# A two-layer diffusion backbone on one core: the first stage of layer 0 gets more places and a merged scale-and-shift pass, and layer 1 computes its input projection with tokens as rows

## The chip, the cores and the metric

The kernel runs on one core of a Trainium2 chip. The engines are TensorE (PE, with its weight loads PEld shown apart), VectorE (DVE), ScalarE (ACT), GpSimd (POOL) and SyncE (SP). SP issues nearly all transfers. The metric is device time of one execution in microseconds. The kernel before has a median of 1796.73 us over three runs (1795.94 to 1799.53).

## The reference, cut to what matters

The input is a latent stream `x` of 256 tokens by 2048 channels, a context stream of the same size and a conditioning vector. Two layers follow each other. Layer 0 mixes with neighbourhood attention and a bidirectional state-space scan, layer 1 with a gated short convolution:

```
for i in range(DEPTH):                                   # DEPTH = 2
    shift, scale, gate = adaln(c, ada_w[i], ada_b[i])
    h = modulate(rms_norm(x, norm_g[i]), shift[:, None], scale[:, None])
    ...
    if i % 2 == 0:  y, yc = na_ssd_mixer(h, hc, ...)     # layer 0
    else:           y = short_conv_mixer(h, sc_w_in, sc_conv_w, sc_w_out)
    x = x + gate[:, None] * y

def short_conv_mixer(h, w_in, conv_w, w_out):
    p = h @ w_in                                         # 256 x 2048 @ 2048 x 8192
    bg, cg, hv, g = jnp.split(p, 4, axis=-1)
    y = bg * dw_conv(cg * hv, conv_w)                    # 3 taps along the tokens
    return (jax.nn.silu(g) * y) @ w_out                  # 2048 x 2048
```

All of it is float32. Shift and scale of layer 0 are needed for the latent stream and for the context stream.

## The kernel before

**Split products.** Each float32 operand of a large product is split into a high part, rounded to the fp32r type, and a low part, the remainder. A product is then three matmuls: high by high, high by low, low by high. Weights arrive by transfers of 512 KB (`raw`, 128 x 1024), ACT makes the high part (`split`, L407) and DVE the low part (`low_part`, L414). There are three places (`NW = 3`) for split weights, used in turn, and five `raw` buffers; during the first stage four more tiles (`spare`: PT0, PT1, xtm, yi) serve as `raw` as well.

**Two forms of a product.** Every matmul is recorded on L189 and every transpose on L193; the profile's names read out<-moving,stationary. In the "act" form (`mm_act`) a 128 x 128 block of activations is stationary, 512 weight columns move, and the result has tokens as partitions: three matmuls of 512 columns for each block of 128 channels, 128 tokens and 512 outputs. In `mm_ws` the weights are stationary. `mm_both` is a variant of it that only layer 1 uses: activations' high and low parts for all 256 tokens lie side by side in one tile of 512 columns, so one matmul of 512 columns with the high weights and one of 256 with the low weights serve a block of 128 channels and 128 outputs. The result has channels as partitions, with the two halves of the bank still to be added (`both`, L1771 and L1773).

**Order of the work.** A planner (`Plan`) keeps a modelled clock of each engine and of the transfers (`RATE`, in bytes per ns) while the program is written out. Generators (`ada_gen`, `res_gen`, `norm_gen` and so on) yield what they wait for, and `pump` or `force` emits their next instructions once the model says that these are ready. The result is one fixed order per engine, and each engine runs its own order strictly in sequence. `keys` says which piece of a tile an access touches, for the model's dependences.

**First stage (L700 to L899).** Eight steps `j`, each for 256 of the 2048 input channels. A step needs its scale and shift: `ada_gen` multiplies the padded conditioning vectors by eight `raw` loads, four for the scale and four for the shift, each part with a bank, an ACT copy, two transposes and a DVE reduction of its own. Then it builds `hH` and `hL` (scaled input, high and low), and PE runs the K, V and Q columns in the act form and the B columns with stationary weights. K and V are summed over the steps on DVE (`part_gen`, L776).

**From layer 0 to layer 1 (L1564 to L1755).** The output projection of layer 0 runs in three passes over 16 chunks; the first pass has two column blocks of 512 and takes its four banks at once. In the last pass the last three chunks (`NTAIL = 13`) are run for tokens 0 to 127 first and then for tokens 128 to 255. `res_gen` forms the residual `x1` and its squares, `turn_gen` transposes `x1` to channels by tokens, `norm_gen` forms the root mean square of each token, spreads it over the partitions with a transpose (bank `rb`), and makes the normalised `h1` channel block by channel block for all 256 tokens together. Two sets of dummy transposes (`keep_up`) run on PE meanwhile. Layer 1's first matmul waits for the first `h1`.

**Layer 1 (L1757 to L1855).** For each of four channel groups `i` the parts 1, 2, 0, 3 of `sc_in` are projected with `mm_both` into four banks, and `cg_gen`, `hv_gen`, `bg_gen` and `gg_gen` do the gating and the convolution in the channel-major layout. Then the output projection runs in the act form, and `fin_gen` writes the result.

Of the kernel before, what the change touches and what calls it, by code (L numbers as in the profile page):

```python
# [15 lines left out]
KB = 16  # L16
# [21 lines left out]
class Plan:  # L38
# [3 lines left out]
    RATE = 270.0  # L42
# [7 lines left out]
    def keys(self, ap):  # L50
        a, n = ap.ap, ap.tensor.name
        if type(ap.tensor).__name__ == "Tile" and not n.startswith("dram"):
            lo = ap.offset % a[0][0] if a[0][0] else ap.offset
            hi = lo + sum(abs(s) * (c - 1) for s, c in a[1:])
            return [(n, u) for u in range(lo // 128, hi // 128 + 1)]
# [86 lines left out]
def kernel(ctx: ExitStack, tc, x, cx, ada0, ada_w, ada_b, w_in, w_out, sc_in, sc_out, rpb, small, const,  # L142
# [27 lines left out]
    KT, QT, Vt, gt = st([128, 4, 512], "KT", F32R), st([128, 4, 256], "QT", F32R), st([128, 4, 512], "Vt"), st([128, 4, 256], "gt")  # L170
    KL, QL = st([128, 4, 512], "KL", F32R), st([128, 4, 256], "QL", F32R)
# [3 lines left out]
    spare = [t.rearrange("p a b -> p (a b)") for t in (PT[0], PT[1], xtm, yi)]  # L175
# [212 lines left out]

    def split():
        k = pos["split"]  # L390
        raw, v = RAW.pop(k)
        nb, n = v.shape[1], v.shape[2]
        if n == 64:
# [3 lines left out]
            W = WH[k % NW].rearrange("p (b c) -> p b c", b=nb)  # L397
# [7 lines left out]
        H = WH[k % NW][:, :nb * n].rearrange("p (b c) -> p b c", b=nb)  # L405
        Lo = WL[k % NW][:, :nb * n].rearrange("p (b c) -> p b c", b=nb)
# [16 lines left out]
    def split_half(b):  # L423
# [5 lines left out]
        def rest():  # L429
            E(V.tensor_tensor(out=Lo[:, b], in0=v[:, b], in1=H[:, b].bitcast(F32), op=ALU.subtract))  # L430
            if b:
                RAW.pop(0)
                HL[0] = (H, Lo)
                pos["split"] += 1
                give_raw(raw)
                issue()
# [3 lines left out]
    def splits_try():  # L440
# [3 lines left out]
        while pos["split"] < pos["use"] + NW and pos["split"] in RAW:  # L444
# [18 lines left out]
    def used():  # L463
        pos["use"] += 1
        splits_try()
# [78 lines left out]
    for i in range(4):  # L544
        for part in (1, 2, 0, 3):
            q_proj(sc_in, part * D + i * 512, 512)
# [103 lines left out]
    def mm_both(ps, act, H, Lo, first, last):  # L650

        for b, o in enumerate(ps):
            bb = slice(b * 128, (b + 1) * 128)
            mm(o, H[:, bb], act, first, False)
            mm(o[:, :256], Lo[:, bb], act[:, :256], False, last)
            if b % 2:
                pump()

    def chunk(kb0, kind, ps, first, last, lhs=None):
# [3 lines left out]
        for j in range(nb):  # L663
# [5 lines left out]
            elif kind == "both":  # L669
                mm_both(ps, aH, H[:, j], Lo[:, j], f, l)  # L670
# [18 lines left out]
    S0 = st([128, KB, 2], "S0")  # L689
    g0 = P_("g0")  # L690

    def ada_gen():
        bc = lambda ap: ap.unsqueeze(2).to_broadcast([128, 2, 2])
        for j in range(8):
            k2 = slice(2 * j, 2 * j + 2)
            for part, dst in ((0, A0), (1, S0)):
                ps = None
                for q in range(4):
                    key = ("ada", j, part, q)
                    w_ = 2 if j == 0 else 4  # L700
                    if q % w_ == 0:
                        ks = [("ada", j, part, q + i) for i in range(w_)]
                        yield when(lambda: all(k in RAW for k in ks))
                        yield W_("PE", *[RAW[k][1] for k in ks], nb=0 if ps is not None else 1)
                    if ps is None:
                        ps = bank()
                    raw, v = RAW.pop(key)
                    for g in range(4):
                        mm(ps[32 * g:32 * g + 32, :256], cpad[:, 4 * q + g, :], v[:, g, :], q == 0, q == 3)
# [3 lines left out]
                Rt = half()  # L713
                E(S.copy(Rt, ps[:, :256]))

                yield W_("PE", Rt)
                for b in range(2):
                    turn(ps[:, 256 + b * 128:384 + b * 128], Rt[:, b * 128:(b + 1) * 128])
                give(free_h, Rt)
                yield W_("DVE", ps)  # L720
                p2 = dst[:, k2, :]
                E(V.tensor_reduce(out=p2, in_=ps[:, 256:].rearrange("p (b g c) -> p b c g", b=2, c=32)[:, :, 0:2, :],
                                  axis=AX.X, op=ALU.add))
                if part == 0:
                    E(V.tensor_tensor(out=dst[:, k2, :], in0=p2, in1=bc(bs1[:, k2]), op=ALU.add))
                    E(V.tensor_tensor(out=dst[:, k2, :], in0=dst[:, k2, :], in1=bc(g0[:, k2]), op=ALU.mult))
                else:
                    E(V.tensor_tensor(out=dst[:, k2, :], in0=p2, in1=bc(P_("ab0")[:, k2]), op=ALU.add))
                give(free_b, ps)

# [169 lines left out]
    force(lambda: all(("part", 7, key, t) in got for key in "KV" for t in range(4)), (urgent,))  # L900
    got.add(("V", 0))
# [661 lines left out]
    x1 = []  # L1563
# [3 lines left out]
    def res_gen(k, c0, ps):  # L1567
# [31 lines left out]
    rb1 = []  # L1599
# [5 lines left out]
    def turn_gen():  # L1605
        yield when(lambda: n_back[0] >= 11.5 and attn[0] == 32 and ssd_done[0] == 8)
        for k in range(2):
            pt = st([128, 4, 256], f"PT{k}", name=f"late{k}")
            late[4 * k:4 * k + 4] = [pt[:, q, :] for q in range(4)]
        E(V.scalar_tensor_tensor(out=A1, in0=M1[:, 1], scalar=1.0, in1=P_("g1"), op0=ALU.add, op1=ALU.mult))  # L1610
        for kp in range(0, KB, 2):
# [21 lines left out]
    def keep_up(n):  # L1633

        pt = bank()
        for _ in range(n):
            turn(pt[:, :128], ident)
        give(free_b, pt)

    s3 = st([128, 2], "s3")  # L1640

    def norm_gen():
# [4 lines left out]
        rb = None  # L1647
        for t in range(2):
# [264 lines left out]
```

## Time and profile before

| what | value |
|---|---|
| median of three runs | 1796.73 us |
| the profiled execution: time, span | 1797.29 us, 1795.5 us |
| PE busy, PEld busy | 98%, 83% of the span |
| DVE, ACT, POOL busy | 72%, 44%, 2% |
| granted clock of TensorE | 1.000 |
| mean transfer rate | 209 GB/s |

The page's columns are microseconds; a busy share is a share of the span. Matmuls are pipelined and their ends are modelled, so the mean duration of one matmul is longer than the distance between two of them. The distance is read from starts, or from the busy time of a dense stretch divided by the number of its matmuls.

### The profile page before, as it was taken

To read this page: it belongs to the slowest core of one execution; us is meant where nothing else is said; L and a number is where in the kernel's file an instruction comes from. 1 tells how busy PE (TensorE), PEld (TensorE's weight loads), DVE (VectorE), ACT (ScalarE), POOL (GpSimd) and SP (SyncE) were. 2 spreads that over 40 slices of the span, in tenths; PEclk is the share of its full clock that TensorE was granted. 3 is DMA by queue.
4 is the path that set the end of the run, shared out by engine and by line. 5 is a ranking of instruction groups with operands and counts; after the bars stand their busy time and mean duration, and the time that the engine had idled before them with its cause. 6 is when DMAs were issued, how large, how long until landed. Compare 5 with 4: busy or idle time off the path is not lost. (4 is left out here: it accounts for less than half of the span.)

```text
span 1795.5 us, 26501 instructions
## 1 busy us (share of the span) xinstructions
PE 1765.5 (98%) x10039; PEld 1490.7 (83%) x10039; DVE 1292.8 (72%) x2073; ACT 786.9 (44%) x1386; POOL 32.5 (2%) x28
## 2 busy tenths in 40 slices
PE   6999999999999999999999999999999999999998
PEld 4677988879888889888888898788888888888887
DVE  5656787888676878676877688786667877565665
ACT  5323544455242445242435344555444444444442
POOL 0000100001000000000001000000000000000000
PEclk9999999999999999999999999999999999999999
DMA  9987744666746665745764567657766786666564
GB/s 359 339 285 239 225 143 125 204 183 200 235 127 202 211 185 175 232 139 173 218 200 134 165 185 247 202 186 268 274 222 225 249 265 222 185 185 187 186 213 150
DMA packets 222368, 374.67 MB, mean 209 GB/s; under 512 B 32432, under 2 KB 69136, under 8 KB 222240
## 3 DMA queue, kind: packets, MB, share of 16 engines
q1 hardware_dynamic: 214928, 366.38, 64.0%
q10 hardware_dynamic: 7312, 6.61, 1.1%
q8 instruction: 78, 1.28, 0.3%
q14 instruction: 50, 0.41, 0.1%
HBM read 367.52 MB, written 6.72 MB: 208 GB/s over the span
## 5 line engine op out<-in xcount | busy, mean ns | idle before, releaser
L407 ACT CAST wH<-raw 128x1024 fp32r<-128x1024 f32 (+1 forms) x439 | 457.8, 1044 | 687.3 <-PE bank L189 561.3
L414 DVE TENSOR_TENSOR wL<-raw,wH 128x1024 fp32r<-128x1024 f32 (+1 forms) x439 | 531.5, 1214 | 250.0 <-ACT wH L407 247.2
L189 PE MATMUL bank<-h,wH 128*128 128x512 f32 x1024 | 362.5, 399 | 1.4 <-DVE h L1669 0.9
L189 PE MATMUL bank<-hH,wH 128*128 128x256 f32 (+1 forms) x1040 | 343.3, 330 | 0.8 <-ACT wH L407 0.8
L189 PE MATMUL bank<-hL,wH 128*128 128x256 f32 (+1 forms) x1040 | 338.0, 325 | 0.0
L189 PE MATMUL bank<-hH,wL 128*128 128x256 f32 (+1 forms) x1024 | 330.8, 323 | 0.8 <-DVE wL L414 0.6
L189 PE MATMUL bank<-h,wL 128*128 128x256 f32 x1024 | 287.6, 281 | 0.0
L189 PE MATMUL bank<-wH,hH 128*128 128x512 f32 x640 | 257.1, 402 | 3.9 <-ACT hH L744 2.6
L189 PE MATMUL bank<-wL,hH 128*128 128x512 f32 x640 | 250.4, 392 | 0.0
L189 PE MATMUL bank<-wH,hL 128*128 128x512 f32 x640 | 249.8, 391 | 0.1
L804 DVE SCALAR_TENSOR_TENSOR acc<-raw,csil,acc 128x512 f32<-128x512 f32 x256 | 191.8, 749 | 63.2 <-DMA raw<-in_ada_w 54.3
L189 PEld LDWEIGHTS bank<-h,wH 128*128 128x128 f32 x1024 | 192.4, 188 | 50.4 <-issue 1.5
L189 PEld LDWEIGHTS bank<-hH,wH 128*128 128x128 f32 x1040 | 196.5, 189 | 18.6 <-ACT wH L407 1.3
L189 PEld LDWEIGHTS bank<-hL,wH 128*128 128x128 f32 x1040 | 196.8, 189 | 15.5
L189 PEld LDWEIGHTS bank<-hH,wL 128*128 128x128 f32 x1024 | 194.0, 189 | 18.3 <-DVE wL L414 1.6
L189 PEld LDWEIGHTS bank<-h,wL 128*128 128x128 f32 x1024 | 193.4, 189 | 0.0
L189 PE MATMUL bank<-wH,mix 128*128 128x512 f32 x512 | 163.1, 393 | 1.1 <-DVE Vt L998 1.1
L189 PEld LDWEIGHTS bank<-wH,hH 128*128 128x128 f32 x640 | 120.2, 188 | 33.8 <-issue 5.0
L189 PEld LDWEIGHTS bank<-wH,hL 128*128 128x128 f32 x640 | 120.2, 188 | 26.1 <-DVE hL L750 0.6
L189 PEld LDWEIGHTS bank<-wL,hH 128*128 128x128 f32 x640 | 120.2, 188 | 24.7 <-DVE wL L430 0.5
L189 PEld LDWEIGHTS bank<-wH,mix 128*128 128x128 f32 x512 | 96.1, 188 | 21.7 <-DVE Vt L998 1.6
L189 PE MATMUL bank<-wL,mix 128*128 128x512 f32 x256 | 100.0, 391 | 0.3 <-DVE wL L414 0.3
(262 smaller groups left out, 1764.0 us busy)
## 6 DMA issues: line engine op xcount, KB each, us to landing
raw<-in_w_in SPq DMA_DIRECT2D x208, 512.0 KB
raw<-in_ada_w SPq DMA_DIRECT2D x128, 512.0 KB
raw<-in_sc_in SPq DMA_DIRECT2D x128, 512.0 KB
raw<-in_w_out SPq DMA_DIRECT2D x64, 512.0 KB
raw<-in_ada SPq DMA_DIRECT2D x37, 512.0 KB
raw<-in_sc_out SPq DMA_DIRECT2D x32, 512.0 KB
tmp<-dram_csr SPq DMA_DIRECT2D x32, 256.0 KB
PT<-in_ada SPq DMA_DIRECT2D x14, 512.0 KB
```

The lines of the kernel that those rows point to most:

```text
L189: E(T.matmul(o, l, r, start=start, stop=stop, skip_group_check=True))
L407: E(S.copy(H, v))
L414: E(V.tensor_tensor(out=Lo, in0=v, in1=H.bitcast(F32), op=ALU.subtract))
L804: E(V.scalar_tensor_tensor(out=acc, in0=v[:, j], scalar=csil[:, 2 * k + j:2 * k + j + 1], in1=acc, op0=ALU.mult, op1=ALU.add))
```

## The change

The planner's transfer rate goes from 270 to 310, and it tracks the small constant tiles in pieces of 2 elements instead of 128.

First stage: `spare` gains six `raw` places, cut from the tiles of KT, KL, QT and QL, which are claimed for their own use only after the stage. A split weight takes any free place (`place`, `free_w`) rather than the next of a ring; in step 0 the place of Q's weights is released early. For steps 2 to 7 `ada_gen` does scale and shift in one run: eight loads together, one bank, one ACT copy of 512, four transposes, one reduction, three additions or multiplications. Steps 0 and 1 stay as they were. The first pass of layer 0's output projection takes its banks two by two.

Into layer 1: three more split places are made from KL, QT, QL, gt and sz after the first pass. `keep_up` goes. `norm_gen` works by token tiles: the factor of tokens 0 to 127 is spread by PE after 15 of the 18 last matmuls of tokens 128 to 255 (`NSTOP`), `h1` of channel blocks 0 to 7 is built for tokens 0 to 127, and layer 1 begins with these eight blocks for tokens 0 to 127, then for tokens 128 to 255, and goes on with blocks 8 to 15 for both.

Layer 1: `mm_both` and `both` go. The projection uses the act form: two banks for a part, tokens as partitions. The parts' order is 1, 2, 3, 0. The product `cg * hv` and the gate's product with `bg` are formed with tokens as partitions, and each is turned to channels by tokens with PE transposes in groups of four (`over`).

```
-    RATE = 270.0
+    RATE = 310.0
...
+    spare = [t.rearrange("p a b -> p (a b)") for t in (PT[0], PT[1], xtm, yi)] + \
+        [st([128, 1024], n, name=f"first{n}") for n in ("QT", "QL")]
+    for n in ("KT", "KL"):
+        kt = st([128, 2, 1024], n, name=f"first{n}")
+        spare += [kt[:, 0], kt[:, 1]]
...
-        while pos["split"] < pos["use"] + NW and pos["split"] in RAW:
+        while free_w and pos["split"] in RAW:
...
+            if j > 1:
+                ks = [("ada", j, part, q) for part in range(2) for q in range(4)]
+                yield when(lambda: all(k in RAW for k in ks))
+                yield W_("PE", *[RAW[k][1] for k in ks], nb=1)
+                ps = bank()
+                for _, _, part, q in ks:
+                    raw, v = RAW.pop(("ada", j, part, q))
+                    for g in range(4):
+                        mm(ps[32 * g:32 * g + 32, part * 256:part * 256 + 256], cpad[:, 4 * q + g, :], v[:, g, :],
+                           q == 0 and part == 0, q == 3)
...
+                if t == 2:
+                    free_w.append(in_use[2])
+                    in_use[2] = None
+                    splits_try()
...
-            yield when(lambda: x1 and (k in passed or ("rows", k, t) in got))
+            yield when(lambda: x1 and (k in passed or ("rows", k, t) in got) and (k < 3 or t == 0 or "first" in got))
...
-                keep_up(8)
-                yield when(lambda: ("sq", 3, 1) in got)
+                yield when(lambda: ("h1", 7, 0) in got)
...
+        yield from factor(0)
+        ahead()
+        yield from spread(0)
+        tt = slice(0, 128)
+        yield W_("DVE", rb[0][:, tt])
+        scaled(0, tt)
+        scaled(2, tt)
+        for kb in range(0, 4):
+            low(kb, tt)
+        scaled(4, tt)
+        got.add("first")
+        yield when(lambda: ("sq", 3, 1) in got)
+        low(4, tt)
+        low(5, tt)
+        scaled(6, tt)
+        yield from factor(1)
...
-        pss = [banks(2) for n in ns]
+        pss = []
...
+            for H, Lo in ((KL[:, 0:2], KL[:, 2:4]), (QT, QL), (st([128, 4, 256], "gt", F32R, name="wH5"), st([128, 4, 256], "sz", F32R, name="wL5"))):
+                free_w.append(len(WH))
...
+    def over(rows_, b):
+        yield W_("PE", *rows_, nb=1)
+        pt = bank()
+        for k in range(2):
+            for t in range(2):
+                turn(pt[:, k * 256 + t * 128:k * 256 + (t + 1) * 128], rows_[t][:, (b + k) * 128:(b + k + 1) * 128])
+        return pt
...
     for i in range(4):
-        for part, gen in ((1, cg_gen), (2, hv_gen), (0, bg_gen), (3, gg_gen)):
-            ps = banks(4)
-            for kb in range(0, KB, 2):
-                force(lambda: hL[kb + 1] is not None)
-                chunk(kb, "both", ps, kb == 0, kb == KB - 2, lambda i: (h1[i], None))
+        for part, gen in ((1, cg_gen), (2, hv_gen), (3, gg_gen), (0, bg_gen)):
+            ps = banks(2)
+            kb0 = 0
+            if i == 0 and part == 1:
+                kb0 = 8
+                ws = []
+                for t in range(2):
+                    for kb in range(8):
+                        force(lambda: ("h1", kb, t) in got, (urgent,))
...
+            for kb in range(kb0, KB, 2):
+                force(lambda: ("h1", kb + 1, 1) in got)
+                chunk(kb, "act", ps, kb == 0, kb == KB - 2, lambda i: h1[i])
```

More of the change, by code (lines that the diff above doesn't have):

```diff
@@ new lines, in pair @@
+        def pair(kp):
+            yield when(lambda: ("turn", kp + 1) in got)
+            yield W_("DVE", r2, held[kp] if kp in held else late[kp])
+            for kb in (kp, kp + 1):
+                if kb not in held:
+                    E(V.tensor_tensor(out=late[kb], in0=late[kb], in1=r2, op=ALU.mult))
+                else:
+                    E(V.scalar_tensor_tensor(out=late[kb], in0=held[kb][:, (kb % 2) * 256:(kb % 2) * 256 + 256],
+                                             scalar=A1[:, kb:kb + 1], in1=r2, op0=ALU.mult, op1=ALU.mult))
+                high(kb, slice(0, 256))
+            if kp in held:
+                give(free_b, held[kp])
+            ahead()
@@ new lines, in norm_gen @@
+        low(7, tt)
+        if lows:
+            low_half(1)
+        yield from spread(1)
+        tt = slice(128, 256)
+        yield W_("DVE", rb[0][:, tt])
+        scaled(0, tt)
+        scaled(2, tt)
+        for kb in range(0, 4):
+            low(kb, tt)
+        scaled(4, tt)
+        scaled(6, tt)
+        r2 = half()
+        E(S.copy(r2, rb[0][:, :256]))
+        ahead()
+        for kb in range(4, 8):
+            low(kb, tt)
+        give(free_b, rb[0])
+        yield from pair(8)
@@ new lines, in ordered @@
+        seq[0] += 1
+    def over(rows_, b):
[5 more added lines that the diff above has]
+        return pt
+    def cg_gen(i, ps):
+        for t in range(2):
+            yield W_("ACT", ps[t])
+            if i == 0:
+                cg.append(tmp())
+            E(S.copy(cg[t], ps[t]))
+            give(free_b, ps[t])
```

338 lines of the change are left out of this document (193 added, 145 removed).

## The prediction

> **What bounds the kernel now.** I read the page first, then the waits of PE, then busy time by stretch.
>
> ```profile
> PE 1765.5 (98%) x10039; PEld 1490.7 (83%) x10039; DVE 1292.8 (72%) x2073; ACT 786.9 (44%) x1386; POOL 32.5 (2%) x28
> PEclk9999999999999999999999999999999999999999
> ```
>
> ```profile
> PE bank L189 <- DMA raw<-in_ada: 11.7, 1, 11.7
> PE bank L189 <- ACT hH L744: 2.6, 2, 1.4
> ...
> PE bank L189 <- DVE Vt L998: 1.1, 1, 1.1
> PE bank L189 <- DVE sz L776: 1.0, 1, 1.0
> ...
> PE bank L189 <- ACT h L1688: 0.5, 1, 0.5
> PE bank L189 <- DVE gt L776: 0.3, 1, 0.3
> ```
>
> PE works through the whole span at the full clock; its waits, fourteen rows, sum to some 24 us, 11.7 of them the first transfer. Only three things can therefore move the end: fewer or denser PE instructions, a shorter hand-over between stages, and fewer stalls of the first stage. Work on ACT and DVE costs nothing unless it holds PE up. The densities, as PE busy time of the instructions on one tile (h is layer 1's input projection, y its output projection, mix layer 0's):
>
> ```profile
> 1337.40:1701.90 364.50, 362.89 (x2048) 1.00 0.67 211
> 1701.80:1789.90 88.10, 87.87 (x384) 1.00 0.57 185
> 1230.00:1330.00 100.00, 98.74 (x434) 1.00 0.78 271
> ```
>
> So a pair of `mm_both` (512 and 256 columns) takes 362.89 / 1024 = 354.4 ns; a matmul of the act form 87.87 / 384 = 228.8 ns in layer 1's output projection and 98.74 / 434 = 227.5 ns in layer 0's.
>
> **The change part by part.** I count against the profiled execution: 1797.29 us, 0.56 above the median.
>
> *A, layer 1's product.* It goes from 1024 pairs to 4 groups x 4 parts x 16 blocks x 2 token tiles x 3 = 1536 matmuls of 512 columns. The nearest rows are the act form's: 1536 x 228.8 = 351.4, or at 227.5, 349.4. Against 362.9 that is -11.5 (bound -13.5); I take the first, since it has layer 1's own output stage with its bank changes. The other bound, nothing gained, is a rival below. The streamed columns stay the same, 1024 x 768 = 1536 x 512; the gain exists only because a pair costs 354.4 where the act form's price per column would make it 343.2.
>
> *B, the transposes that the token-major form needs.* `over` is called twice in `hv_gen` and twice in `bg_gen` for each of four groups: 16 groups of four. The timeline has one such group inside the act form:
>
> ```profile
> 1181.52 0.39 PE L189 MATMUL bank<-wH,mix 128*128 128x512 f32 x1
> 1181.75 0.60 PE L193 MATMUL bank<-const,tmp 128*128 128x128 f32 x4
> 1182.11 0.48 PE L189 MATMUL bank<-wH,mix 128*128 128x512 f32 x1
> 1182.42 0.39 PE L189 MATMUL bank<-wL,mix 128*128 128x512 f32 x1
> ```
>
> From the matmul before it to the second one after it are 0.90 us where two matmuls take 0.46, so a group costs 0.44 and 16 cost +7.0 (each matmul after it is slower once, which is in this figure). The removed `both` additions, 64 on ACT and 64 on DVE, and the new gating lie beside PE: DVE has 28% of the span free. I cost them at nothing; without that cover a part of 22 us (8 chunks x 12 x 0.229) would have to hold more than 22 us of DVE work, and its 8 low parts are
>
> ```profile
> L414 DVE TENSOR_TENSOR wL<-raw,wH 128x1024 fp32r<-128x1024 f32 x432 | 526.7, 1222 | 249.2 <-ACT wH L407 246.5
> ```
>
> 8 x 1.22 = 9.8; the heaviest gating, `hv`, adds two products of 512 columns (0.69, as L1585 below) and eight taps of 255 (0.48, as L1669 below), 5.2 us. The changed order of the parts costs nothing.
>
> *C, the entry to layer 1.* Before, in the timeline of PE:
>
> ```profile
> 1331.98 0.39 PE L189 MATMUL bank<-wH,mix 128*128 128x512 f32 x1
> ...
> 1333.97 0.33 PE L193 MATMUL bank<-const,x1b 128*128 128x128 f32 x1 [0.61 <-DVE x1b L1585]
> ...
> 1334.79 1.04 PE L193 MATMUL bank<-const 128*128 128x128 f32 x8
> ...
> 1337.51 0.50 PE L189 MATMUL bank<-h,wH 128*128 128x512 f32 x1 [0.92 <-DVE h L1669]
> ```
>
> From the last matmul's end of stream (1331.98 + 0.23) to layer 1's first are 5.3 us, with 16 needed transposes of `x1` (four groups, 1.8 us), two that spread the factors, and 14 dummies; the wait of 0.5 for `h1` (h L1688 above) comes later. After the change the transposes stay (1.8 + 0.3), and PE has 24 matmuls (5.5 us) of tokens 0 to 127 while the factor of tokens 128 to 255 is made. The chain that decides is now DVE's:
>
> ```profile
> 1330.42 0.21 DVE L1652 TENSOR_SCALAR r<-ss,s 128x1 f32<-128x1 f32 x1 [0.79 <-ACT tmp L1589]
> 1331.36 1.23 DVE L414 TENSOR_TENSOR wL<-raw,wH 128x1024 fp32r<-128x1024 f32 x1 [0.73 <-ACT wH L407]
> 1332.50 0.68 DVE L1582 TENSOR_TENSOR tmp<-bank,tmp 128x512 f32<-128x512 f32 x1
> 1333.22 0.69 DVE L1585 TENSOR_TENSOR x1b<-tmp,tmp 128x512 f32<-128x512 f32 x1
> ```
>
> The first factor (1330.63 on DVE, then POOL) is on PE before the last three matmuls end; its scaling, high and low part put the first `h1` near 1333, when the transposes of blocks 8 to 11 end. But within the 5.5 us of tokens 0 to 127 DVE has more to do. What a scaling and a low part of 256 columns take there:
>
> ```profile
> 1342.12 0.42 DVE L1681 TENSOR_TENSOR late<-late,half 128x256 f32<-128x256 f32 x1
> 1342.45 0.48 DVE L1669 SCALAR_TENSOR_TENSOR h<-late,M,h 128x256 fp32r<-128x256 f32 x1
> 1342.85 0.42 DVE L1681 TENSOR_TENSOR late<-late,half 128x256 f32<-128x256 f32 x1
> ```
>
> From start to start 0.33 and 0.40; a low part of 128 columns I put at 0.27 (between half and all of 0.40). Four scalings (1.3), eight low parts (2.2), the second residual (1.4) and two or three weights' low parts (1.2 each) are 7 to 8.5 us against 5.5, so I expect 1.5 to 3 us of waiting. That is 2.1 + 2.2 = 4.3 us against 5.3 + 0.5: -1.5, between -4 (no waiting) and +2 (DVE is late twice, at blocks 0 to 7 and again at 8 to 15).
>
> *D, the first stage.* Merging scale and shift for steps 2 to 7 leaves the same 64 matmul instructions, but one batch for two:
>
> ```profile
> 91.69 0.40 PE L189 MATMUL bank<-wL,hH 128*128 128x512 f32 x1
> 92.02 0.64 PE L189 MATMUL bank<-xtm,cpad 128*32 128x256 f32 x8
> 92.48 1.05 PE L189 MATMUL bank<-raw,cpad 128*32 128x256 f32 x16
> 93.34 0.61 PE L189 MATMUL bank<-PT,cpad 128*32 128x256 f32 x8
> 93.89 0.50 PE L189 MATMUL bank<-wH,hH 128*128 128x512 f32 x1
> 94.23 0.39 PE L189 MATMUL bank<-wH,hL 128*128 128x512 f32 x1
> ```
>
> 2.54 us from first to last, less two matmuls (0.46) and four eights (0.43 each from 92.48 to 93.34): 0.36 us of entry and exit, saved six times: -2.1. Four transposes together cost 0.44, as two pairs do, so they bring nothing. Stalls: the longest after 40 us are
>
> ```profile
> 50.48 0.50 PE L189 MATMUL bank<-hH,wH 128*128 128x512 f32 x1 [0.83 <-ACT wH L407]
> 51.47 0.50 PE L189 MATMUL bank<-hH,wL 128*128 128x512 f32 x1 [0.26 <-DVE wL L414]
> 86.96 0.51 PE L189 MATMUL bank<-wH,hH 128*128 128x512 f32 x1 [1.00 <-DVE sz L776]
> ```
>
> The first two are B's weights of step 0, whose split had no place while K, V and Q held all three; the early release takes that wait away, about -1. The third is DVE late with a bank, because `h` of the next step is made just in time. The places bear on that through the transfers:
>
> ```profile
> 20.00:40.00 20.00, 16.39 (x100) 11.00 (x104) 13.08 (x35) 13.72 (x31) 1.61 (x4) 1.00 1.05 395
> 40.00:60.00 20.00, 18.91 (x182) 12.87 (x178) 12.23 (x31) 9.43 (x22) 0.00 (x0) 1.00 0.94 338
> 70.00:75.00 5.00, 5.00 (x47) 3.20 (x46) 2.08 (x3) 1.47 (x3) 0.00 (x0) 1.00 0.47 148
> ```
>
> Up to 60 us the transfer engines are full, so nothing comes sooner there. Later they drop to 148 GB/s for want of places, yet PE is busy 5.00 of 5.00 in that stretch: the drop itself is hidden. What more places and the planner's faster rate can do is bring the next step's scale, shift and `h` forward and take the 1.0 and the 0.3 (gt above) before it: -0.9, less about 0.5 for new waits behind the longer batch. D is -3.5, between -8 and +2.
>
> *E.* At the first pass of layer 0's output projection PE waited 1.1 for the fourth bank (Vt L998 above). Two by two, the second pair is chosen a chunk later; the copy that frees it is no earlier. -0.5, between -1.1 and +0.5. The finer dependence tracking and the new order of everything between move stalls of a few tenths: 0, within 1.5 either way.
>
> Sum: -11.5 + 7.0 - 1.5 - 3.5 - 0.5 = -10.0, so 1787.3 for the profiled execution and 1786.7 on the median; the rivals' times are on the median too.
>
> **The rivals.**
>
> *The pair's price stays in the token-major form.* If the 354.4 ns come from layer 1's surroundings (weights arriving, the gemv on DVE) and not from the 256-column matmul, time per column stays and A is 0: 1786.7 + 11.5 = 1798.2, no change. For it: no row shows the act form in this place. Against: both other projections, with the same weight stream, have 228. A price between, 232, would give 1791.6.
>
> [...]
>
> *The merged batch stalls PE (ends slower).* PE takes its order strictly; a batch of eight loads emitted at a modelled 310 GB/s waits for the eighth. A load of 512 KB takes 1.55 us at the 338 GB/s of 40 to 60 us. Two loads late in each of six steps cost 18.6: 1805.3. It decides from 1.7 us a step (10.0 / 6). For it: delivery of 338 leaves little over 310. Against: PE, not transfers, is the bound after 60 us, and six more places let them run ahead.
>
> *DVE holds the entry.* In the 22.6 us after layer 1's start DVE was busy 21.11:
>
> ```profile
> 1337.40:1360.00 22.60, 22.00 (x122) 18.72 (x123) 21.11 (x40) 15.07 (x24) 0.00 (x0) 1.00 0.48 146
> ```
>
> Halving the tiles adds about 1.2 us of DVE work. If its queue decides, C is +2 and the time 1790.2. Without `keep_up` PE may then stand still for some us in a row.
>
> [...]
>
> *The first stage gives all it has.* If its stalls after 33 us vanish, D is -8 and the time 1782.2.
>
> **How the numbers follow.** Forecast 0.56 (1783 to 1790); first stage gives all 0.12; DVE holds the entry 0.14; pair's price stays 0.09; batch stalls 0.07; other losses 0.02. The likeliest gives 1786.7. The range from 1778.5 (A -13.5 with D -8 and C -3) to 1796 leaves out the batch's stall, most of the unchanged case and a little below. A measurement tells about 0.2%, 3.6 us, from no change: faster is forecast, full first stage and entry, 0.82; same 0.10; slower 0.08.
>
> **What would show it.** Layer 1's matmuls on h: 1536, PE busy near 351 without the transposes; groups of four `const,tmp` transposes, 16 of them; the gap from the last mix to the first h matmul below 2.5 us; batches of 64 `cpad` instructions six times; output projection of layer 0 reached some 3 us earlier. Wrong if the act form's matmuls on h stand over 232 ns apart, if PE's waits show `raw<-in_ada` between 60 and 160 us, or if DVE `h` or `late` appears in them for more than 3 us.

## The result: 0.25% slower, and where the time went

The changed kernel takes 1800.5 us in the median (1796.6 to 1804.1), the kernel before, beside it, 1795.9 (1793.6 to 1799.5). The ratio is 1.0025, interval 1.0019 to 1.0031: slower by 4 to 5 us where 10 us less were forecast. The profiled execution has a span of 1800.5 us and a mean granted clock of 0.996; before had 1.000.

The page's first part after the change, and its largest waits of PE apart from the first transfer and `hH`, which are as before (us in total, times, longest). In the changed kernel matmuls stand on L193 and transposes on L197:

```profile
PE 1766.4 (98%) x9577; PEld 1475.6 (82%) x9577; DVE 1263.9 (70%) x1980; ACT 772.4 (43%) x1324; POOL 31.3 (2%) x28
```

```profile
PE bank L193 <- DVE gt L809: 2.4, 2, 1.8
PE bank L193 <- DVE half L1474: 2.4, 1, 2.4
PE bank L197 <- POOL r L1689: 2.1, 1, 2.1
PE bank L193 <- DVE tmp L1445: 1.7, 2, 1.1
PE bank L193 <- ACT Vt L1037: 1.6, 1, 1.6
PE bank L197 <- DVE sgH L1938: 1.3, 1, 1.3
```

PE issues 462 instructions fewer and is busy 0.9 us longer. Apart from the first transfer, before had no wait over 1.4 us; now there are several of 1.6 to 2.4.

By stage, from the starts of PE's instructions in the two profiled executions: the first stage (to the first matmul for the G columns) takes 198.4 us (198.5 before); from there to layer 1's first matmul on h 1148.1 (1139.0), which is the loss; layer 1's input projection 359.9 (364.4), which is the gain; the output projection 88.6 (87.9).

The gain is seen on the tile h, where 1024 pairs with 362.9 us became this (PE busy, number, clock):

```profile
1320.00:1710.00 390.00, 353.24 (x1536) 1.00 0.65 208
```

The loss is seen first at the clock. Busy time of PE in stretches of 3.41 us (length, PE busy and number, granted clock, transfers):

```profile
87.12:90.53 3.41, 1.68 (x8) 1.00 1.01 377
90.53:93.95 3.42, 3.35 (x14) 1.00 1.07 408
404.57:407.98 3.41, 1.19 (x6) 1.00 0.97 324
407.98:411.40 3.42, 3.29 (x10) 0.50 0.11 44
1339.82:1343.23 3.41, 1.41 (x7) 1.00 0.98 324
1343.23:1346.64 3.41, 3.30 (x13) 0.50 0.33 125
```

After the waits of 2.4 us (from 405.8) and 2.1 us (from 1341.2) the clock is halved, for 6.83 us from 407.98 and for 3.41 us from 1343.23; behind the 1.7 us of idleness at 87 it is not. The stretches at half clock are 13.7 us in all up to 1347 us (3.4 of them in the first stage, at 25.7), which by an estimate at half speed costs up to 6.8 us, 1.7 for each 3.41 us. The wait at 1341 stands in the timelines of PE and of DVE:

```profile
1340.84 0.39 PE L193 MATMUL bank<-wH,mix 128*128 128x512 f32 x1
1343.34 0.48 PE L197 MATMUL bank<-const,r 128*128 128x128 f32 x1 [2.11 <-POOL r L1689]
...
1344.47 0.63 PE L193 MATMUL bank<-wH,mix 128*128 128x512 f32 x1
...
1346.46 0.57 PE L193 MATMUL bank<-wH,h 128*128 128x512 f32 x1
```

```profile
1336.63 0.75 DVE L837 SCALAR_TENSOR_TENSOR acc<-raw,csil,acc 128x512 f32<-128x512 f32 x1 [6.02 <-DMA raw<-in_ada_w]
1337.31 1.22 DVE L425 TENSOR_TENSOR KL<-raw,KL 128x1024 fp32r<-128x1024 f32 x1
1338.44 0.74 DVE L837 SCALAR_TENSOR_TENSOR acc<-raw,csil,acc 128x512 f32<-128x512 f32 x1
1339.10 1.22 DVE L425 TENSOR_TENSOR QL<-raw,QT 128x1024 fp32r<-128x1024 f32 x1
1340.24 0.68 DVE L1621 TENSOR_TENSOR tmp<-bank,tmp 128x512 f32<-128x512 f32 x1
...
1342.44 0.21 DVE L1688 TENSOR_SCALAR r<-ss,s 128x1 f32<-128x1 f32 x1 [0.52 <-ACT tmp L1628]
```

DVE stood 6.0 us before a load of the gemv (the modulation of layer 1), with two low parts and the residual `x1a` queued behind it; the token factor `r` came late and PE waited. The waits alone do not make up the loss. From the first G matmul to the last mix the changed kernel takes 12.7 us longer, and from there to the first h 3.5 less. Of the 12.7 some 4.5 are added waits and some 4.0 the half clock (8.1 us of it there). The rest is spread over the body: matmuls of 512 columns on hH and hL that follow one another without a break start 231.4 ns apart there in the mean, where before they start 229.5 ns apart, and there are some 2340 of them, another 4.5 us. The operands have the same shapes, but the tiles hH8 to hH15, hL0 and hL1 lie elsewhere: with more places for loads the x loads claim their tiles earlier, and the 32 bytes of the new tile AS come ahead of hL0.

### The profile page after: what moved, and what is told of

Read it like the earlier page. It is cut to its first block, busy times and chain, and to the rows that moved or that the text cites. A ratio compares the mean times of both kernels' runs of the same rounds, so it can differ in the third digit from the quotient of the medians.

```text
span 1800.5 us, 25364 instructions
## 1 busy us (share of the span) xinstructions
PE 1766.4 (98%) x9577; PEld 1475.6 (82%) x9577; DVE 1263.9 (70%) x1980; ACT 772.4 (43%) x1324; POOL 31.3 (2%) x28
## 4 chain that ended last, share of the span: by engine, by line
PE 79%; DMA 7%; DVE 4%; issue 1%; ACT 1%; SPq 0%; POOL 0%; DVEq 0%; ACTq 0%
PE bank L193 76%; DMA raw<-in_ada_w 4%; PE bank L197 3%; DMA tmp<-dram_csr 2%; DVE acc L837 1%; DVE wL L425 1%; DMA tmp<-dram_mixd 1%; DMA raw<-in_w_out 1%; ACT wH L418 0%; DVE QL L425 0%; DVE KL L425 0%; ACT tmp L1425 0%; DVE tmp L1429 0%; DVE acc L823 0%; DVE tmp L1621 0%
## 5 line engine op out<-in xcount | busy, mean ns | idle before, releaser
L418 ACT CAST wH<-raw 128x1024 fp32r<-128x1024 f32 (+1 forms) x363 | 380.5, 1049 | 583.9 <-PE bank L193 503.1
L425 DVE TENSOR_TENSOR wL<-raw,wH 128x1024 fp32r<-128x1024 f32 (+1 forms) x362 | 440.1, 1219 | 209.6 <-ACT wH L418 205.3
L193 PE MATMUL bank<-hH,wH 128*128 128x256 f32 (+1 forms) x1040 | 344.0, 331 | 0.0
L193 PE MATMUL bank<-hL,wH 128*128 128x256 f32 (+1 forms) x1040 | 338.7, 326 | 0.0
L193 PE MATMUL bank<-hH,wL 128*128 128x256 f32 (+1 forms) x1024 | 330.4, 323 | 0.4 <-DVE wL L425 0.4
L193 PE MATMUL bank<-wH,hH 128*128 128x512 f32 x640 | 259.6, 406 | 4.9 <-ACT hH L777 2.6
L837 DVE SCALAR_TENSOR_TENSOR acc<-raw,csil,acc 128x512 f32<-128x512 f32 x256 | 191.8, 749 | 87.3 <-DMA raw<-in_ada_w 77.1
L193 PE MATMUL bank<-wL,hH 128*128 128x512 f32 x640 | 252.8, 396 | 0.0
L193 PE MATMUL bank<-wH,hL 128*128 128x512 f32 x640 | 251.8, 394 | 0.1
L193 PE MATMUL bank<-wH,h 128*128 128x512 f32 x680 | 216.2, 391 | 0.0
L193 PEld LDWEIGHTS bank<-hH,wH 128*128 128x128 f32 x1040 | 195.4, 188 | 19.1 <-issue 1.4
L193 PEld LDWEIGHTS bank<-hL,wH 128*128 128x128 f32 x1040 | 195.8, 188 | 16.2
L193 PEld LDWEIGHTS bank<-hH,wL 128*128 128x128 f32 x1024 | 193.2, 189 | 18.5 <-DVE wL L425 0.6
L193 PEld LDWEIGHTS bank<-wH,h 128*128 128x128 f32 x680 | 127.8, 188 | 26.9 <-issue 0.2
L193 PEld LDWEIGHTS bank<-wH,hH 128*128 128x128 f32 x640 | 121.4, 190 | 34.1 <-issue 3.4
L193 PEld LDWEIGHTS bank<-wH,hL 128*128 128x128 f32 x640 | 121.2, 190 | 27.7 <-DVE hL L783 0.6
L193 PEld LDWEIGHTS bank<-wL,hH 128*128 128x128 f32 x640 | 121.3, 190 | 25.2 <-DVE wL L425 0.4
L193 PE MATMUL bank<-wH,mix 128*128 128x512 f32 x432 | 138.2, 394 | 1.6 <-ACT Vt L1037 1.6
L193 PE MATMUL bank<-wL,h 128*128 128x512 f32 x340 | 132.6, 390 | 0.0
L193 PEld LDWEIGHTS bank<-wH,mix 128*128 128x128 f32 x432 | 81.5, 189 | 19.3 <-ACT Vt L1037 2.1
L193 PE MATMUL bank<-wL,mix 128*128 128x512 f32 x216 | 84.9, 393 | 0.6 <-DVE wL L425 0.6
L193 PEld LDWEIGHTS bank<-wL,h 128*128 128x128 f32 x340 | 63.9, 188 | 13.2
```

What stands on the lines that cost most here:

```text
L193: E(T.matmul(o, l, r, start=start, stop=stop, skip_group_check=True))
L418: E(S.copy(H, v))
L425: E(V.tensor_tensor(out=Lo, in0=v, in1=H.bitcast(F32), op=ALU.subtract))
L837: E(V.scalar_tensor_tensor(out=acc, in0=v[:, j], scalar=csil[:, 2 * k + j:2 * k + j + 1], in1=acc, op0=ALU.mult, op1=ALU.add))
```

## The experiments

Ratios are to the kernel before on the same chip; a difference in us is a difference of ratios times 1795.9. Three theories: the *addresses* slow the matmuls; the *order* that the planner writes with the rate 310 brings the waits; the *clock* multiplies them. Their rival is that a part of the change itself costs more than forecast.

### Addresses alone

a1, the changed kernel; b1, the kernel before with the changed kernel's addresses; b2, before with even ones. No engine's instructions or order change.

```
a1  -    x_load(0); x_load(1); issue(); bs1 = st([128, 16], "bs1")
    +    bs1 = st([128, 16], "bs1"); x_load(0); x_load(1); issue()
    -    AS = st([128, 4, 2], "AS")          # moved to its first use
b1  +    for k in range(8, 16): st([128, 512], f"hH{k}", name=f"claim{k}")   # ahead of bs1
    +    st([128, 4, 2], "AS")
b2  the first edit of a1, in the kernel before
```

> The changed kernel with nothing but two tiles allocated at another moment: bs1 (64 bytes a partition) ahead of the first x loads, AS (32 bytes) at its first use. Every engine issues the same instructions in the same order; only addresses differ: the tiles hH, hL (and what later takes their places, mix, h1, y2) begin at multiples of 128 bytes within a partition instead of 64 or 32 beyond one. Theory of addresses: in the trace of the changed kernel a matmul of 512 columns starts 227.1 ns after the one before where both operands and the next ones are at multiples of 128, 229.6 where the stationary one is 64 beyond, 232.8 at 32 beyond, 234.6 to 235.9 where the moving one alternates between 0 and 64. Weighted by how often each occurs this is some 14 us: 1786 us, and the waits of the body stay where they are. Theory of order (the planner's new order alone costs the time): same instructions, same order, so 1800, within 1.5. Theory of the clock (waits over 2 us, then half clock for 3.4 or 6.8 us): the clock drops at about 26, 408 and 1343 us stay, as the order is the same, and so the time is 1800 unless the addresses matter too.

> The kernel before with the addresses of the changed kernel: places of hH8 to hH15 claimed ahead of bs1, and 32 bytes claimed ahead of hL0; the same instructions in the same order. Theory of addresses: by the same distances, slower than before by 7 to 8 us, 1803. Theory of order or of the clock: no change, 1796, within 1.5.

> The kernel before with bs1 allocated ahead of the first x loads, so that all hH begin at multiples of 128 bytes; the same instructions in the same order. Theory of addresses: faster than before by 6 to 7 us, 1789. Theory of order or of the clock: no change, 1796, within 1.5.

Measured: a1 1791.5 us, ratio 0.9971 (0.9960 to 0.9983), 9.7 us less than the changed kernel; b2 1793.1, 0.9980 (0.9972 to 0.9989), 3.6 less than before; b1 1796.4, 0.9997 (0.9988 to 1.0007), no difference. So a shift of 32 or 64 bytes moves the time of an unchanged list of instructions, but by less than expected in a1 (some 14) and b2 (6 to 7), and not at all in b1. In a1 and b2 the pace accounts for it: on hH and hL the starts are 227.6 ns apart in both, 3.9 less than in the changed kernel and 2.0 less than before, over some 2350 matmuls 9.0 and 4.6 us.

b1 tells why not. Its matmuls of 512 columns in the body are slower as expected (231.4 ns apart against 229.5), but layer 1's pairs became faster, with the same addresses relative to 256 bytes in 14 of the 16 h tiles and 32 bytes more in two:

```profile
1344.70:1703.20 358.50, 356.73 (x2048) 1.00 0.69 214
```

A pair takes 356.73 / 1024 = 348.4 ns there, against 354.4 before. In the starts, before repeats three pairs (241 + 120, 236 + 113, 233 + 117 ns, from the wider to the narrower and on), b1 nearly always one (230 + 117). The same stream has two rhythms; what starts the one or the other stays open. In b1 layer 1 takes 5.9 us less, which hides the 5.6 us that its body takes more. The token-major form has no such pairs, so nothing hid the price in the changed kernel.

a1 kept its waits and got longer ones, with the clock halved behind them; its twelve executions run from 1786.7 us at a mean clock of 0.999 to 1798.8 at 0.993, and a line through them falls 1.9 us for each 0.001.

### The planner's rate

a2 is a1 with 270 throughout; c1 is a1 with 310 for the first stage and 270 behind it; d3 and d4 are c1 with 240 and 290 there; d2 is b2 (before, even) with 310 behind the first stage.

```
a2  -    RATE = 310.0
    +    RATE = 270.0
c1       got.add(("V", 0))
    +    plan.RATE = 270.0        # d3: 240.0, d4: 290.0; d2, in before: 310.0
```

> The kernel a1 (changed kernel, even addresses) with the planner's transfer rate back at 270, which changes the order that it writes for all engines. Theory of order (an optimistic rate lets PE arrive at weights, at csr and at the gemv's loads before they have landed): the waits of 2.4 us at 405 and of 2.1 us before layer 1 shrink below 1, and with them the drops of the clock go; 6 to 10 us less than a1. If the order is a lottery that the rate does not aim: within 4 us of a1 on either side, with drops at other places.

> The changed kernel with even addresses (a1) and the planner's rate at 310 until the first stage has been written and 270 from there. The trace of a1 reaches the first G matmul at 197.2 us against 203.6 with 270 throughout; from there to the end it needs 1594 against 1573.5. Theory of order (the faster rate is right where the stage is bound by transfers and wrong behind it): the first stage of the one and the rest of the other, 1783.8 - 6.5 = 1777. Lottery (any new order draws its own waits): between 1778 and 1791 with waits over 1 us at new places.

> The kernel before with even addresses (b2, 1793.1) with the rate at 270 in the first stage and 310 behind it: nothing of the change but the rate that the planner works with in the body. If an optimistic rate makes PE arrive ahead of transfers in any kernel: slower by 8 to 15, 1801 to 1808, with waits of DVE for the gemv's loads above the 62 us of b2. If the loss of 15 us belongs to the change's own order and another draw would do as well: between 1789 and 1797.

> c1 (1776.2) with the rate behind the first stage at 240 instead of 270. If the planner's rate has only to be low enough that loads have landed when an instruction is written for them: 1776, from 1774 to 1779. If each rate is a draw of its own: up to 8 us above or below.

> c1 (1776.2) with the rate behind the first stage at 290, between c1 and a1 (310, 1791.5). If the loss grows with the rate: about half of it, 1781 to 1786. If each rate is a draw of its own: anywhere from 1774 to 1791.

Measured:

| kernel | rate behind the first stage | us | ratio | interval |
|---|---|---|---|---|
| a2 (270 in the first stage too) | 270 | 1783.8 | 0.9930 | 0.9918 to 0.9941 |
| d3 | 240 | 1791.0 | 0.9978 | 0.9970 to 0.9987 |
| c1 | 270 | 1776.2 | 0.9888 | 0.9873 to 0.9903 |
| d4 | 290 | 1783.2 | 0.9938 | 0.9925 to 0.9950 |
| a1 | 310 | 1791.5 | 0.9971 | 0.9960 to 0.9983 |
| d2 (before) | 310 | 1789.6 | 0.9972 | 0.9961 to 0.9984 |

c1 is as expected and beats both kernels. But the theory that an optimistic rate makes PE early in any kernel falls twice: in the kernel before 310 costs nothing (d2, within the interval of b2), and a lower rate, 240, costs as much as 310 (d3). d4 alone (290, between c1 and a1) would also fit a loss that grows with the rate; d3 does not fit it. Each rate writes another order, and each order has its own few waits or none. c1's waits of PE, complete from 1 us up, are those of the first stage alone:

```profile
PE bank L193 <- DMA raw<-in_ada: 11.9, 1, 11.9
PE bank L193 <- ACT hH L779: 2.6, 2, 1.4
PE bank L193 <- DVE gt L811: 2.5, 2, 1.8
PE bank L197 <- ACT half L749: 1.0, 2, 0.5
```

### The changed kernel with one line more

d1 is the changed kernel with its own addresses and the line of c1: the same order as c1.

> The changed kernel itself, its addresses as they are, with one line more: the planner's rate goes from 310 to 270 once the first stage has been written. Its instructions and their order are those of c1 (1776.2). If the losses are the rate behind the first stage (a1 1791.5 against c1 1776.2: 15.3) and the addresses (after 1800.5 against a1 1791.5: 9.0) and these add: 1776.2 + 9 = 1785, from 1783 to 1787. If the addresses cost only where the order is the one of 310: under 1780.

Measured: 1787.6 us, 0.9958 (0.9945 to 0.9972), 12.6 us above c1, where 9 was expected and a1 had shown 9.7. The addresses' price is there in this order too and adds to the order's. It is seen best where both run the same 162 matmuls (hH, hL moving, weights stationary) without a break; first d1, then c1:

```profile
807.14:845.13 37.99, 37.99 (x165) 1.00 0.69 211
```

```profile
802.33:839.07 36.74, 36.74 (x164) 1.00 0.68 212
```

The stretches begin and end with the same instructions (the counts include the one or two still running at their edges): 37.98 us against 36.75 from the first start to the one behind the last, 234.4 ns each against 226.8, with PE busy all the time at the full clock. By operands, in the changed kernel's trace: 227.1 ns where all begin at multiples of 128 bytes, 229.6 where the stationary one is 64 beyond, 234.6 to 235.9 where moving operands at 0 and at 64 beyond alternate. The pace is measured, its mechanism is not.

### The parts of the change by themselves

Both on b2 (1793.1), with even addresses. c2 has layer 1's part, its entry and the banks two by two; c3 the first stage's places, the merged scale and shift, and 310 until the stage is written, without the early release of Q's place.

```
c2  the diff without: RATE, keys, spare, ada_gen, the early release in step 0
c3  only: keys, spare, ada_gen, RATE = 310.0 and plan.RATE = 270.0 behind the stage
```

> Layer 1's part alone, on the kernel before with even addresses (b2, 1793.1): token-major product, its entry, banks two by two, parts 1 2 3 0; the first stage, its places, the scale and shift batches and the rate of 270 are those of before, and PE's order is that of before up to layer 0's output projection. My sums: product and transposes -4.5 (A and B; by a1's trace 1536 x 227.0 + 16 x 0.44 against 1024 x 353.3, -6.1), entry -1.5 as forecast (by a2's trace, 1.0 instead of 5.5 us between the last mix and the first h, -4.5), banks -0.5: 1786.6 as forecast, 1782 by the traces of a1 and a2. Theory of the clock: within this, plus 1.7 for each wait over 2 us. Rival that layer 1 itself brings the loss: over 1793.

> The first stage's part alone, on the kernel before with even addresses (b2, 1793.1): places for loads in QT, QL, KT, KL, merged scale and shift for steps 2 to 7, rate 310 until the stage has been written and 270 behind it; without the early release of Q's place. As forecast for D without its release: -2.5, 1790.6. By a1's trace (197.2 against 198.3 at the first G matmul): -1, 1792. Rival that the merged batch stalls PE: over 1796 with waits of raw<-in_ada behind 60 us. Lottery of what follows in the body: 2 either way on each.

Measured: c2 1781.3 us, 0.9915 (0.9901 to 0.9928), 11.7 less than b2; c3 1787.1, 0.9949 (0.9936 to 0.9961), 5.6 less. Together they would give 17.3; c1, which has both, is 16.5 below b2. So neither part loses by itself; the early release, and each piece within a part, was not run alone. In c2 the entry is 1.0 us where before had 5.5 (last mix to first h):

```profile
1328.22 0.39 PE L189 MATMUL bank<-wH,mix 128*128 128x512 f32 x1
1328.45 0.27 PE L193 MATMUL bank<-const,x1a 128*128 128x128 f32 x1
...
1329.24 0.48 PE L189 MATMUL bank<-wH,h 128*128 128x512 f32 x1
```

Of c3's 5.6 us the first stage itself gave nothing in its profiled execution (198.4 us to the first G matmul, 198.3 in b2): without the early release PE waited 2.2 us for B's first weights (`ACT wH L411`), with the clock halved behind it (0.997 in the mean of that execution). In c1, with the release, the stage takes 196.6, which is 1.7 less. c3's gain lies in the order that follows: from the first G matmul to the last mix it takes 1124.0 us, b2 1128.8.

### The clock

c4 is b2 without the 14 dummy transposes of `keep_up`.

```
-                keep_up(8)
-        keep_up(6)
```

> The kernel before with even addresses (b2, 1793.1) without the 8 and 6 dummy transposes at the entry to layer 1, which leave PE idle some 2.4 of the 2.7 us from 1329.9 to 1332.6. Theory of the clock (drops begin on a grid of 3.413 us, in the window behind one in which PE was idle for more than about 1.6 us): a stretch of 3.4 us at half clock at about 1333 in most runs, and +1.7 in each that has it: 1794.5. If waits do not bear on the clock: 1793.1, within 1, clock 1.00 there.

```profile
1326.99:1330.40 3.41, 1.31 (x8) 1.00 0.53 154
1330.40:1333.81 3.41, 2.92 (x9) 0.50 0.00 0
1333.81:1337.23 3.42, 3.42 (x22) 0.99 0.64 183
```

The stretch at half clock is there, in the 3.41 us that follow a stretch with 2.1 us of idleness. The grid in the expectation is that of the changed kernel's drops, at 25.68, 407.98 and 1343.23 us; its limit of some 1.6 us was the author's estimate, and that trace does not bear it out: behind 1.59 us of idleness the clock was 0.50 at 25.68 and 1.00 at 1442.22, and behind 1.73 us, at 90.53, it was 1.00. The time is 1791.5, 0.9975 (0.9965 to 0.9984), where 1794.5 was expected, and not above b2: its executions run from 1789.7 to 1794.5 us, and in the profiled one a wait of 1.2 us that b2 has at 583 us is absent. So the drop is shown by this run, and its price is not; the price rests on the line through a1's executions.

### What the waits of the losing orders hang on

f1 to f3 are a1, f4 is d3, with an eighth of the bytes in the gemv's loads, in the csr rows (the decay rows of the state-space heads) or in both. The order is kept, since the planner is told the full size. These kernels leave out seven eighths of that data.

```
f1  -    E(DMA.dma_start(v, w[r0:..., c0:c0 + n]))             # gemv loads
    +    E(DMA.dma_start(v[:, :, :64], w[r0:..., c0:c0 + 64]), v)
f2  -    E(DMA.dma_start(two(rw), ... [1, 256]))               # csr rows
    +    E(DMA.dma_start(two(rw)[:, :, :32], ... [1, 32]), two(rw))
    -    E(S.activation(Dm, Dm, AF.Exp))
    +    E(S.activation(Dm, Dm, AF.Identity))
f3, f4  both
```

> a1 (changed kernel, even addresses, rate 310 throughout, 1791.5) whose gemv loads bring 64 of 512 columns, an eighth of the bytes; the planner is told the full size, so every engine's order stays as in a1. It leaves out most of the gemv's weights: the modulation of layer 1 is computed from what lies in the places. If late transfers make the waits: those that hang on raw<-in_ada_w, before layer 1 (3.5 us, POOL r) and at 1435 (2.6, DVE sgH), go, the csr waits at 403 and 1143 shrink as they no longer queue behind these loads: 1779 to 1784. If the queues of ACT and DVE make them: the waits stay above 2 us and the time is 1788 to 1793.

> a1 with the csr loads bringing 32 of 256 columns, an eighth of the bytes, and a copy in place of the exponential behind them; same order as in a1. It leaves out most of the decay rows of the state-space heads. If the size of the csr transfers makes them late: the waits at 403 and 1143 go below 1 us, those at 1335 and 1435 stay: 1783 to 1787. If they are late because they queue behind the 512 KB loads issued ahead of them: ACT still waits over 4 us for tmp<-dram_csr at 400 and 1135, and the time is 1789 to 1792.

> a1 with both cuts, same order. If late transfers make all four waits: none of them above 1 us from 200 us on, the clock full from 30 us on, and the time is that of c1, 1776 to 1779. If something else is left: the waits show where.

> d3 (rate 240 behind the first stage, 1791.0) with both cuts, same order as d3. There PE waits for the weights' high and low parts (QT, KL, wL) at 1329 and 1335 while DVE is idle only for engines: if these come of the order on DVE and ACT and of no transfer, they stay, and the time falls by less than 4: 1787 to 1791. If a transfer is behind them too: 1776 to 1780.

a1's waits of PE, and the one of ACT that stands behind `half` and `Vt`:

```profile
PE bank L197 <- POOL r L1691: 3.5, 1, 3.5
PE bank L193 <- DVE half L1476: 3.2, 1, 3.2
PE bank L193 <- ACT Vt L1039: 3.0, 1, 3.0
PE bank L193 <- DVE tmp L1447: 2.8, 2, 2.0
PE bank L197 <- DVE sgH L1940: 2.6, 1, 2.6
```

```profile
ACT tmp L1427 <- DMA tmp<-dram_csr: 27.8, 13, 6.6
```

f1 takes 1782.8 us, 0.9936 (0.9919 to 0.9952): the waits for `r` and `sgH` are gone, `half` and `Vt` fell to 0.9 and 1.2, and the longest left is 2.7 us at 396, behind a csr load that held ACT for 5.2 us until 392. f2 takes 1780.3, 0.9922 (0.9907 to 0.9936), below the 1783 to 1787 expected: `half`, `Vt` and `tmp` are gone, two waits stay, though shorter, and ACT still stands before a csr load, at most 4.0 us instead of 6.6:

```profile
PE bank L197 <- POOL r L1692: 1.9, 1, 1.9
PE bank L197 <- DVE sgH L1941: 1.5, 1, 1.5
ACT tmp L1428 <- DMA tmp<-dram_csr: 11.5, 6, 4.0
```

f3 takes 1773.5, 0.9879 (0.9864 to 0.9893), a little below the 1776 to 1779 expected. This is all that PE waits for in it, none of it behind 160 us, and the clock is 1.000:

```profile
PE bank L193 <- DMA raw<-in_ada: 11.6, 1, 11.6
PE bank L193 <- ACT hH L781: 2.6, 2, 1.4
PE bank L193 <- DVE gt L813: 2.5, 2, 1.9
PE bank L197 <- ACT half L751: 1.0, 2, 0.5
PE bank L197 <- ACT xs L611: 0.7, 1, 0.7
```

So in a1's order, which is the changed kernel's, late transfers make the waits: the csr rows those at 403 and 1143 us, the gemv's weights those at 1335 and 1435. The two are not independent: with the gemv's bytes cut alone the csr waits shrink, and with the csr bytes cut alone the gemv's do. How much of a csr load's lateness is its size and how much the loads ahead of it is not separated: ACT's longest wait fell from 6.6 to 4.0 us with an eighth of the bytes. f4 takes 1784.1, 0.9939 (0.9924 to 0.9954), 7 us less than d3, where less than 4 was expected; there the wait at 1135 went, and those at the entry stayed as they were (`ACT QT`, 3.8 us in d3):

```profile
PE bank L193 <- ACT QT L420: 3.9, 1, 3.9
PE bank L193 <- DVE KL L427: 1.8, 1, 1.8
```

At a rate of 240 the entry loses through the order on ACT and DVE, not through one of these transfers: ACT splits QT's weights behind `h` blocks for which it waits on DVE. So the two losing orders lose in different ways.

## Why the prediction was wrong, step by step

With even addresses on both sides the change as written is worth 1.6 us (a1 against b2, within their intervals no difference), and in the order of c1 16.5 (c1 against b2); the forecast sum was 10.0. Of the 16.5, 4.2 lie between the first G matmul and the last mix, where the sum had only E's 0.5: c1's order is a lucky one there. What came, slower, had been given 0.08, nearly all of it for the merged batch stalling PE, which did not happen. The low end of the range is 1778.7 by its own terms, not 1778.5, which changes nothing.

- **A and B, product and transposes.** Forecast -11.5 and +7.0, so -4.5. In the changed kernel the input projection fell from 364.4 to 359.9 us, -4.5, with 1.6 us of waits for `sgH` and `sgL` in it; in c2 it is 357.6 against b2's 364.3, -6.7. The matmuls start 227.7 ns apart in the changed kernel and 226.9 in c2, where 228.8 was taken. Right in mechanism and size, with A near its bound of -13.5. The rival that the pair's price stays is refuted. That the price of a pair was not fixed (354.4 or 348.4 ns) was not foreseen.
- **C, the entry.** Forecast -1.5, "between -4 (no waiting) and +2". Without late loads it is -4.5 (c2), a little beyond the bound. In the changed kernel the distance from mix to h is 2.0 us, as the forecast's sign "below 2.5" wanted, but a wait of 2.1 us and half a clock moved ahead of it. DVE did hold the entry, not by its halved tiles, as the rival had it, but by standing before a gemv load.
- **D, the first stage.** Forecast -3.5. It is -0.2 in the changed kernel and -1.7 in c1, where the stage's stretch at half clock is absent; inside the range, the term too large. More places and the faster rate were to take away the waits for `sz` and `gt`, 1.3 us together; in the changed kernel the wait for `gt` is 2.4 instead. No `raw<-in_ada` appears among PE's waits after the first, so the merged batch does not stall PE.
- **E, banks two by two.** Forecast -0.5. Before waited 1.1 us for the fourth bank (Vt L998), c2 waits 0.8, c1 not at all, the changed kernel 1.6, with ACT 4.2 us behind a csr load at 1143 and not caught up by then. Right in size where ACT is on time.
- **The failed step** is "The finer dependence tracking and the new order of everything between move stalls of a few tenths: 0, within 1.5 either way". The new order cost 14.9 us (a1 against c1). It was read as small because before's waits were small; but they were small in that one order, and ACT and DVE already stood before the same loads in it (before, waits of ACT, then of DVE):

```profile
ACT tmp L1386 <- DMA tmp<-dram_csr: 20.9, 13, 5.9
```

```profile
DVE acc L804 <- DMA raw<-in_ada_w: 54.3, 38, 4.1
```

In the changed kernel these are 26.7 and 77.1 us. They were the rows to read, with the question how much work lies ready between them and PE. Their totals alone do not tell it: c1 has 22.5 and 65.1 us, and behind 160 us no wait of PE over 1 us.
- **A term that was not in the sum**: addresses. 9.7 us in the changed kernel, 3.6 in before, +6.1 net. Together: -16.5 + 14.9 + 6.1 = +4.5 us, the measured 0.25%. This sum closes by the way its terms are taken and proves nothing; what shows the terms are a1, c1 and f1 to f3.

The sum had no term for the clock, which fell after waits of 2.4 and 2.1 us. One stretch of 3.41 us at a clock of 0.50 lowers the mean of some 1800 us by 0.00095, and its estimated 1.7 us agree with the line through a1's executions, 1.9 us for each 0.001 of mean clock. The starts of the drops at 25.68, 407.98 and 1343.23 us in the changed kernel are 112.0 and 274.0 times 3.413 us apart.

## What to carry to other kernels

A change to a kernel whose order is written by a planner redraws every wait behind it, and here that was worth as much as the change itself: forecast the parts, then give the order a term of its own, as wide as the idle times of the engines next to PE allow, and try several planner settings before judging the change. Compare the operands' addresses of two builds before comparing their times: small tiles of 32 and 64 bytes, allocated ahead of the large ones, cost up to some 8 ns per matmul here (234.4 ns in d1, 226.8 in c1), and moving the allocation gave them back. Changed kernel, even addresses and a rate of 310 for the first stage and 270 behind it make 1776.2 us, 1.1% faster than before.

## What the runs showed of the hardware

- **The drops of the granted clock lay on a grid of 3.413 us.** In the changed kernel's trace they last 3.41, 6.83 and 3.41 us, at 0.50; in the eleven of the 18 profiled executions that have more than one drop, the drops lie a whole number of such windows apart. Of the 18 executions' windows between 19 us and the last matmul, 14 had PE idle for 1.9 us or more (busy by the modelled ends), and the window behind each of the 14 ran at half clock (in the changed kernel 2.2 us idle from 404.57 and 2.0 from 1339.82, in c4 2.1 from 1326.99); with 1.44 to 1.9 us idle 8 of 24 did (in the changed kernel the one from 22.27, not those from 87.12 and 1438.81); of 9234 windows with less, only four were followed by half clock, and these four ran at half clock themselves (in the changed kernel the one from 407.98). That where the grid cuts a wait near 2 us makes it cheap or dear is the author's estimate from these counts. That the cut moves from execution to execution would fit a1's mean clocks, 0.993 to 0.999 in twelve executions, but only one of these was profiled.
- **The same 162 matmuls ran at two paces with operands at different addresses**: 226.8 ns in c1 against 234.4 in d1, at the full clock, with every operand at a multiple of 128 bytes in c1 and the moving operand alternating between 0 and 64 bytes beyond in d1.
- **One stream of matmuls ran at two paces**: layer 1's pairs at 354.4 ns in the kernel before and 348.4 in b1, with the same instructions; what decides between them is open.
